# One first load for three x tiles, a cast moved to GpSimd, and the last stores cut in other places

## The chip, the cores and the metric

The kernel runs on one core of one Trainium2 chip. The metric is the device time of one execution in microseconds (us). The profile of an execution covers its span from the first to the last instruction, about 2 us less than the time. "Before" is the tuned kernel, "after" the same with the change. A DMA has "landed" when all the engines that move it have reported; each such report is a "landing mark".

## The reference

A batched matrix product with a bias and a residual. The batches fold into one matrix of 8192 x 1024.

```python
batch, m, k, n = 16, 512, 1024, 768
x: (batch, m, k)   weight: (k, n)   bias: (n)   residual: (batch, m, n)     # all float32
return (np.matmul(x, weight) + bias + residual).astype(np.float32)
```

## The kernel before

The 8192 rows are 64 tiles of 128 rows, and eight tiles make a "super tile" (S): partition p of super tile S holds eight neighbouring rows. For each tile, x is cast to bf16, transposed on TensorE in pairs (as fp32), copied back from PSUM (the memory that TensorE writes), multiplied in 16 matmuls, and finished by adds on VectorE and GpSimd. Almost every DMA is issued by SyncE on one queue, in the order of the program. The parts that the change and the argument touch:

```python
P, J, HEAD, X_BUFS, RO_BUFS, EARLY = 128, 8, 3, 2, 4, 24
...
    def store(S, j0=0, j1=J, n0=0, nl=N):
        K_(nc.sync.dma_start(
            out=out_d[S, :, j0:j1, n0:n0 + nl], in_=ro[S][:, j0:j1, n0:n0 + nl]
        ))
...
    load_x(0, 0, 2)          # tiles 0 and 1: 8 KB of each partition
    load_x(0, 2, 3)          # tile 2: 4 KB
    load_w(0)                # then four weight chunks, the rest of x, the residuals
...
    keep_warm(12)            # matmuls on zeros until x is there
    cast(0, "dve")
    cast(1)                  # ACT
    transp(0)
    transp(1)
    keep_warm(3)
    cast(2)                  # ACT
    transp(2)
    # then the bias is broadcast by four matmuls, then the first real matmuls
...
    for t in range(HEAD, n_t):
        ...
        if S == n_s - 1 and j == 0:
            store(S - 1)
        if S == n_s - 1 and j == J // 2:
            store(S, 0, J // 2)          # tiles 0-3 of the last super tile: 1536 KB
        if S == n_s - 1 and j == J - 1:
            store(S, J // 2, j)          # tiles 4-6: 1152 KB
    ...
        store(S, J - 1, J, n0, nl)       # tile 7: 256 KB and 128 KB
```

Of the kernel before, what the change touches and what calls it, by code (L numbers as in the profile page):

```python
# [11 lines left out]
J = 8  # L12
# [9 lines left out]
def kernel(  # L22
# [8 lines left out]
    nc = tc.nc  # L31
# [7 lines left out]
    n_s = n_t // J  # L39
# [12 lines left out]
    def ring(pool, name, i, n, shape, dt):  # L52
        return pool.tile(shape, dt, name=name, tag=f"{name}{i % n}", bufs=1)
# [8 lines left out]
    def load_x(S, j0=0, j1=J):  # L62
        if S < n_s:
            if j0 == 0:
                x_sb[S] = ring(sb, "x_tile", S, X_BUFS, [P, J, K], FP32)
            K_(nc.sync.dma_start(out=x_sb[S][:, j0:j1, :], in_=x_d[S, :, j0:j1, :]))

    def load_res(S, j0=0, j1=J):
        if S < n_s:
            if j0 == 0:  # L70
                ro[S] = ring(sb, "ro", S, RO_BUFS, [P, J, N], FP32)
            K_(nc.sync.dma_start(out=ro[S][:, j0:j1, :], in_=res_d[S, :, j0:j1, :]))

    def load_w(c):
        K_(nc.sync.dma_start(out=w_st[:, c, :, :], in_=w_d[:, c, :, :]))
# [7 lines that stand above are left out]
    def cast(t, engine="act"):  # L83
        if t < n_t:
            xb[t] = ring(sb, "xb", t, 4, [P, K], BF16)
            copy = nc.scalar.copy if engine == "act" else nc.vector.tensor_copy
            K_(copy(out=xb[t], in_=x_sb[t // J][:, t % J, :]))  # L87

    def transp(t):
        if t < n_t:  # L90

            pt = ring(ps, "pt", t, 2, [P, n_c, P], FP32)
            pairs = xb[t][:, :].bitcast(FP32)
            for c in range(n_c):
                K_(nc.tensor.transpose(  # L95
                    out=pt[:, c, :], in_=pairs[:, c * P:(c + 1) * P], identity=ident
                ))
            xt[t] = ring(sb, "xt", t, 4, [P, n_c, P], FP32)
            K_(nc.vector.tensor_copy(out=xt[t], in_=pt))  # L99
# [9 lines left out]
    def mms(t, i):  # L109
        if i == 0:  # L110
            po[t] = psum_o(t)
        for n0, nl in chunks:
            mm(t, i, n0, nl)
# [4 lines left out]
    def pool_add(t):  # L118
        if 0 <= t < n_t:
            r = row(t)  # L120
            K_(nc.gpsimd.tensor_add(out=r, in0=r, in1=tmp[t] if t < EARLY else bias_sb))  # L121

    def finish(t, n0=0, nl=N):
        if t < 0:
            return
        p = po[t][:, n0:n0 + nl]
        if t < EARLY:
            tmp[t] = ring(sb, "tmp", t, TMP_BUFS, [P, N], FP32)
            K_(nc.vector.tensor_add(out=tmp[t], in0=p, in1=bias_sb))  # L129
        else:  # L130
            K_(nc.vector.tensor_add(out=row(t, n0, nl), in0=p, in1=row(t, n0, nl)))  # L131
# [5 lines left out]
    w_st = ring(sb, "ro", RO_BUFS - 1, RO_BUFS, [P, n_c, 2, N], FP32)  # L137
    w_sb = const.tile([P, n_c, 2, N], BF16, name="w_sb")

    load_x(0, 0, 2)  # L140
    load_x(0, 2, 3)
    load_w(0)
    load_w(1)
    load_w(2)
# [23 lines left out]
    def keep_warm(n):  # L168
        for _ in range(n):
            K_(nc.tensor.matmul(  # L170
                warm_ps[:, 0:512], lhsT=warm[:, 0:P], rhs=warm, start=True, stop=True
            ))
# [5 lines left out]
            K_(nc.vector.tensor_copy(out=w_sb[:, c, e, :], in_=w_st[:, c, e, :]))  # L178


    keep_warm(12)
    cast(0, "dve")
    cast(1)
    transp(0)
    transp(1)
    keep_warm(3)
    cast(2)
    transp(2)
    for n0, nl in chunks:
        K_(nc.tensor.matmul(  # L190
# [23 lines left out]
    for t in range(HEAD, n_t):  # L214
        cast(t + 2)
        S, j = divmod(t, J)
        if (t + 2) % J == J - 1:
            load_x(S + X_BUFS)
            load_res(S + X_BUFS)
            if 1 <= S < n_s - 1:  # L220
                store(S - 1)
        if t < n_t - 1:
            for i in range(len(steps)):
                mms(t, i)
                if i == 0 and t >= n_t - J // 2:
                    finish(t - 1)
                if i == T_STEP:
                    transp(t + 1)
        if t < n_t - J // 2 or t == n_t - 1:
            finish(t - 1)  # L230
        if t - 1 < EARLY:
            pool_add(t - 1)
        if t + 1 >= EARLY:
            pool_add(t + 1)
        if S == n_s - 1 and j == 0:
            store(S - 1)
        if S == n_s - 1 and j == J // 2:
            store(S, 0, J // 2)
        if S == n_s - 1 and j == J - 1:
            store(S, J // 2, j)  # L240
    t, S = n_t - 1, n_s - 1
    for b, (n0, nl) in enumerate(chunks):
        po[t] = psum_o(t + b)
# [34 lines left out]
```

## Time and profile before

| | before |
|---|---|
| time, median of 3 runs | 211.06 us (210.88 to 211.19) |
| span of the profiled run | 209.1 us |
| first real matmul, last matmul's end | 10.04, 204.43 us |
| last store issued, last packet's end, last landing | 204.92, 207.78, 208.18 us |

First the page: busy time and share of the span of PE (TensorE's matmuls), and from the 40 equal slices the busy tenths of PE and of the 16 DMA engines.

```profile
PE 201.1 (96%) x1274; PEld 130.8 (63%) x1299; DVE 105.0 (50%) x139; ACT 68.0 (33%) x68; POOL 115.6 (55%) x71
...
PE   7999999999899999999999999999999999999991
...
DMA  6999999999999999999999999999999999999966
```

PE and DMA are both nearly full from beginning to end. Shares alone don't say which of the two decides. Next, groups of instructions: line, engine, operation, tiles and shapes, count, then busy us and mean ns of one, then the engine's idle time and what ended it.

```profile
L87 ACT CAST xb<-x_tile 128x1024 bf16<-128x1024 f32 x62 | 63.2, 1045 | 115.5 <-PE pt L95 63.2
L121 POOL TENSOR_TENSOR ro<-ro,bias_sb 128x768 f32<-128x768 f32 x40 | 71.2, 1816 | 34.6 <-DMA ro<-in_residual_dram 24.6
```

ACT casts a tile in 1.05 us, a GpSimd add takes 1.82 us, and both engines are idle for long.

The chain of waits, in order of time (start, us, what), around the only place where PE stands still for more than 0.14 us after its start:

```profile
22.74 33.22 DMA x_tile<-in_x_dram
...
56.05 1.05 ACT xb L87
...
57.15 0.66 PE pt L95 x4
```

The third x super tile is issued at 22.74 and lands only at 55.95 us, because the queue ahead of it is long. The cast follows, and then the transposition of tile 16. In the records of the transpositions each tile starts 3.037 us after the one before; tile 16 is 0.83 us late and tile 17 another 0.06. From there PE runs without a stall until 204.43.

The head, by the timeline (start, us, engine, line, operation, out<-in, count, idle before and what ended it):

```profile
5.62 1.04 ACT L87 CAST xb<-x_tile 128x1024 bf16<-128x1024 f32 x1 [2.11 <-DMA x_tile<-in_x_dram]
5.62 0.69 DVE L87 CAST xb<-x_tile 128x1024 bf16<-128x1024 f32 x1 [4.35 <-DMA x_tile<-in_x_dram]
...
6.87 1.05 ACT L87 CAST xb<-x_tile 128x1024 bf16<-128x1024 f32 x1 [0.20 <-DMA x_tile<-in_x_dram]
...
8.31 0.60 PE L95 MATMUL pt<-ident,xb 128*128 128x128 f32 x4
...
10.04 1.14 PE L104 MATMUL po<-w_sb,xt 128*128 128x512 bf16 x6
```

The two casts at 5.62 wait for the load of tiles 0 and 1, the cast at 6.87 for the load of tile 2. The first real matmul (line 104) starts at 10.04.

The tail, by DMA issue (KB, then us from issue to landing):

```profile
out_dram<-ro SPq DMA_DIRECT2D x1, 1536.0 KB, 10.4
out_dram<-ro SPq DMA_DIRECT2D x1, 1152.0 KB, 4.2
...
out_dram<-ro SPq DMA_DIRECT2D x1, 256.0 KB, 3.4
out_dram<-ro SPq DMA_DIRECT2D x1, 128.0 KB, 3.3
```

And by windows of half a microsecond; the last two columns are the mean busy share of the 16 DMA engines and what they moved:

```profile
202.50:203.00 0.50, 0.50 (x4) 0.23 (x3) 0.40 (x1) 0.00 (x0) 0.00 (x0) 1.00 0.12 49
203.00:203.50 0.50, 0.50 (x4) 0.26 (x3) 0.00 (x0) 0.00 (x0) 0.00 (x0) 1.00 0.12 49
...
206.50:207.00 0.50, 0.00 (x0) 0.00 (x0) 0.00 (x0) 0.00 (x0) 0.00 (x0) 1.00 0.82 311
207.00:207.50 0.50, 0.00 (x0) 0.00 (x0) 0.00 (x0) 0.00 (x0) 0.00 (x0) 1.00 1.03 369
207.50:208.00 0.50, 0.00 (x0) 0.00 (x0) 0.00 (x0) 0.00 (x0) 0.00 (x0) 1.00 0.33 107
```

A share of 0.12 is 2 of 16 engines. From 202.5 to 203.5 two engines still work while fourteen have nothing to do. The trace also has the 16 landing marks of each of these DMAs, one for each engine. They are the finest view that we have (us from the span's start, sorted):

```
before, store of tiles 0-3:      201.21 201.25 201.30 201.54 201.78 201.91 202.63 202.73 202.84 202.91 202.92 202.97 203.10 203.44 204.16 204.30
before, store of tiles 4-6:      206.92 ... 207.12
before, last store (128 KB):     207.95 ... 208.18
```

Six engines lead, eight are about 1.5 us behind them, two about 3 us. The two laggards never run dry: their last 12 KB packet of the first store ends at 203.83, and the 9 KB packets of the next follow until 206.75. The other fourteen begin the next store at 203.75, having waited for it. So here all engines happen to end together.

Among the packets are ten of 16,384 bytes that belong to no tensor but to the instruction stream, about one every 19 us, each of about 1.0 to 1.1 us on one engine. The Trainium skill ("Runtime: NRT & Kernel Launch", Instruction fetch mechanics) describes instruction refills in blocks of 16 KiB, 256 instructions; ten blocks agree with the 2,573 matmuls and weight loads of this trace. After the first such packet, at 21.98 us, one landing mark of the next DMA is 1.05 us behind the others; after the second there are two such marks, after the third three. But the fetches are not the whole lag. At the store of tiles 0 to 3 the lags behind the first engine add up to 21.6 us. At 20.6 us, before the first fetch, they were 3.7. The ten packets, with four more of 8 KB of the instruction stream, took 11.8 us, so at least about a third of the growth has another cause.

### The profile page before, as it was taken

The page shows a single profiled execution, that of the slowest core. Times are in us where ns is not written, and L with a number is a line of the kernel's source. Part 1 is how long each engine was busy: PE and PEld are TensorE (multiplying, and loading weights), DVE is VectorE, ACT ScalarE, POOL GpSimd, SP SyncE. Part 2 cuts the span into 40 slices and gives each one's busy share as a digit, 9 for nine tenths or more (in the row PEclk, how much of TensorE's full clock was granted, in tenths as well). Part 3 has the DMA queues.
Part 4 walks back from the last instruction along what each step waited for, and adds up shares of the span by engine and source line. Part 5 has one row for each costly group of instructions (what it writes and reads, how often), then busy time and mean ns, then how long its engine had stood idle before and what let it go on. Part 6 is the DMA issues. An engine that isn't in the chain of part 4 may idle for free.

```text
span 209.1 us, 3149 instructions
## 1 busy us (share of the span) xinstructions
PE 201.1 (96%) x1274; PEld 130.8 (63%) x1299; DVE 105.0 (50%) x139; ACT 68.0 (33%) x68; POOL 115.6 (55%) x71
## 2 busy tenths in 40 slices
PE   7999999999899999999999999999999999999991
PEld 2556666666566666666666666666666666666660
DVE  0646564455354455445545544554554455446551
ACT  2544315520283054323423252440543234322000
POOL 2000197819936655999499802994069900799000
PEclk9999999999999999999999999999999999999999
DMA  6999999999999999999999999999999999999966
GB/s 229 428 422 432 430 421 438 443 456 407 404 476 420 409 432 412 443 428 434 437 415 459 415 414 447 437 426 418 428 431 443 445 412 421 432 442 423 414 287 273
DMA packets 5344, 87.23 MB, mean 417 GB/s; under 512 B 593, under 2 KB 721, under 8 KB 1618
## 3 DMA queue, kind: packets, MB, share of 16 engines
q1 hardware_dynamic: 5328, 87.03, 97.8%
q8 instruction: 10, 0.16, 0.3%
q14 instruction: 4, 0.03, 0.0%
q10 hardware_dynamic: 2, 0.00, 0.0%
HBM read 61.87 MB, written 25.17 MB: 416 GB/s over the span
## 4 chain that ended last, share of the span: by engine, by line
PE 70%; DMA 25%; issue 1%; ACT 1%; DVE 0%; POOL 0%; ACTq 0%; POOLq 0%
PE po L104 60%; DMA x_tile<-in_x_dram 23%; PE pt L95 10%; DMA tmp<-in_bias_dram 2%; ACT xb L87 1%; DVE ro L131 0%; POOL ident masks.py:197 0%; ACTq L87 0%; POOL tmp L135 0%; POOLq L262 0%
## 5 line engine op out<-in xcount | busy, mean ns | idle before, releaser
L104 PE MATMUL po<-w_sb,xt 128*128 128x512 bf16 (+1 forms) x999 | 175.4, 324 | 1.4
L104 PEld LDWEIGHTS <-xt 128*128 128x128 bf16 x1024 | 100.1, 98 | 59.5 <-DVE xt L99 0.5
L87 ACT CAST xb<-x_tile 128x1024 bf16<-128x1024 f32 x62 | 63.2, 1045 | 115.5 <-PE pt L95 63.2
L121 POOL TENSOR_TENSOR ro<-ro,bias_sb 128x768 f32<-128x768 f32 x40 | 71.2, 1816 | 34.6 <-DMA ro<-in_residual_dram 24.6
L99 DVE COPY xt<-pt 128x512 f32<-128x512 f32 x64 | 44.2, 692 | 88.3 <-PE pt L95 88.2
L121 POOL TENSOR_TENSOR ro<-ro,tmp 128x768 f32<-128x768 f32 x24 | 43.1, 1816 | 42.3 <-DMA ro<-in_residual_dram 25.0
L131 DVE TENSOR_TENSOR ro<-po,ro 128x768 f32<-128x768 f32 (+2 forms) x41 | 38.0, 930 | 2.9 <-PE po L104 2.8
L95 PE MATMUL pt<-ident,xb 128*128 128x128 f32 x256 | 38.6, 274 | 0.7 <-ACT xb L87 0.7
L95 PEld LDWEIGHTS pt<-ident,xb 128*128 128x128 f32 x256 | 30.1, 142 | 9.2 <-ACT xb L87 1.3
L129 DVE TENSOR_TENSOR tmp<-po,bias_sb 128x768 f32<-128x768 f32 x24 | 22.8, 949 | 0.4 <-PE po L104 0.4
L170 PE MATMUL po<-warm 128*128 128x512 bf16 x15 | 6.1, 579 | 1.2 <-DVE warm L156 1.2
L176 ACT CAST w_sb<-ro 128x768 bf16<-128x768 f32 x4 | 3.3, 832 | 4.0 <-DMA ro<-in_weight_dram 4.0
L170 PEld LDWEIGHTS <-warm 128*128 128x128 bf16 x15 | 1.9, 132 | 4.1 <-issue 2.8
L87 DVE CAST xb<-x_tile 128x1024 bf16<-128x1024 f32 x2 | 1.4, 694 | 5.1 <-DMA x_tile<-in_x_dram 5.1
L178 DVE CAST w_sb<-ro 128x768 bf16<-128x768 f32 x4 | 2.2, 556 | 2.2 <-DMA ro<-in_weight_dram 2.2
L161 ACT ACT_TABLE_LOAD x1 | 1.3, 1283 | 2.0 <-POOL ident masks.py:199 2.0
L190 PE MATMUL po<-tmp 128*128 128x512 f32 (+1 forms) x4 | 1.5, 486 | 0.0
L198 DVE COPY bias_sb<-po 128x768 f32<-128x768 f32 x1 | 1.0, 958 | 0.1
L190 PEld LDWEIGHTS po<-tmp 128*128 128x128 f32 x4 | 0.7, 190 | 0.5 <-issue 0.5
L135 POOL MEMSET tmp<- 128x768 f32 x1 | 0.7, 737 | 0.3 <-POOLq L262 0.3
L156 DVE MEMSET warm<- 128x256 uint32 x1 | 0.3, 272 | 0.9 <-PEq L262 0.9
masks.py:199 POOL TENSOR_SCALAR_AFFINE_SELECT ident<-ident 128x128 f32<-128x128 f32 x1 | 0.3, 292 | 0.1
(8 smaller groups left out, 1.0 us busy)
## 6 DMA issues: line engine op xcount, KB each, us to landing
x_tile<-in_x_dram SPq DMA_DIRECT2D x6, 4096.0 KB, 29.4
ro<-in_residual_dram SPq DMA_DIRECT2D x7, 3072.0 KB, 18.0
out_dram<-ro SPq DMA_DIRECT2D x7, 3072.0 KB, 24.9
x_tile<-in_x_dram SPq DMA_DIRECT2D x2, 2048.0 KB, 23.9
x_tile<-in_x_dram SPq DMA_DIRECT2D x3, 1024.0 KB, 8.7
ro<-in_weight_dram SPq DMA_DIRECT2D x4, 768.0 KB, 9.1
ro<-in_residual_dram SPq DMA_DIRECT2D x2, 1536.0 KB, 20.9
out_dram<-ro SPq DMA_DIRECT2D x1, 1536.0 KB, 10.4
```

The costliest lines, as they stand in the source:

```text
L87: K_(copy(out=xb[t], in_=x_sb[t // J][:, t % J, :]))
L95: K_(nc.tensor.transpose(out=pt[:, c, :], in_=pairs[:, c * P:(c + 1) * P], identity=ident))
L99: K_(nc.vector.tensor_copy(out=xt[t], in_=pt))
L104: K_(nc.tensor.matmul(po[t][:, n0:n0 + nl], lhsT=both[:, e, :], rhs=w_sb[:, c, e, n0:n0 + nl], start=(i == 0), stop=(i == len(steps) - 1),))
L121: K_(nc.gpsimd.tensor_add(out=r, in0=r, in1=tmp[t] if t < EARLY else bias_sb))
L129: K_(nc.vector.tensor_add(out=tmp[t], in0=p, in1=bias_sb))
L131: K_(nc.vector.tensor_add(out=row(t, n0, nl), in0=p, in1=row(t, n0, nl)))
L161: K_(nc.scalar.copy(out=warm_a, in_=warm_a))
L170: K_(nc.tensor.matmul(warm_ps[:, 0:512], lhsT=warm[:, 0:P], rhs=warm, start=True, stop=True))
L176: K_(nc.scalar.copy(out=w_sb[:, c, e, :], in_=w_st[:, c, e, :]))
L178: K_(nc.vector.tensor_copy(out=w_sb[:, c, e, :], in_=w_st[:, c, e, :]))
L190: K_(nc.tensor.matmul(bias_ps[:, n0:n0 + nl], lhsT=ones, rhs=bias_row[:, n0:n0 + nl], start=True, stop=True,))
```

## The change

The intent: fewer and larger packets for the first tiles, with three engines casting at once; and at the end less left to store after the last matmul.

```diff
-    load_x(0, 0, 2)
-    load_x(0, 2, 3)
+    load_x(0, 0, 3)
...
-    keep_warm(12)
+    keep_warm(14)
     cast(0, "dve")
     cast(1)
     transp(0)
     transp(1)
-    keep_warm(3)
-    cast(2)
+    keep_warm(1)
+    cast(2, "pool")                      # nc.gpsimd.tensor_copy
     transp(2)
...
+        if S == n_s - 1 and j == J - 2:
+            store(S, J // 2, j)          # tiles 4 and 5: 768 KB
         if S == n_s - 1 and j == J - 1:
-            store(S, J // 2, j)
+            store(S, j - 1, j)           # tile 6: 384 KB
```

More of the change, by code (lines that the diff above doesn't have):

```diff
@@ L85, in cast @@
             xb[t] = ring(sb, "xb", t, 4, [P, K], BF16)
-            copy = nc.scalar.copy if engine == "act" else nc.vector.tensor_copy
+            copy = {
+                "act": nc.scalar.copy, "dve": nc.vector.tensor_copy,
+                "pool": nc.gpsimd.tensor_copy,
+            }[engine]
             K_(copy(out=xb[t], in_=x_sb[t // J][:, t % J, :]))
```

## The prediction

> **What bounds the kernel now.** Two resources are full at once. The page shows PE busy 96% and the DMA engines at 417 GB/s, slices at 9 almost throughout. The spacing of the transposes in the timeline is 3.04 us per tile with one exception: tile 16 starts 0.83 us late (plus 0.06 at the next). The chain of waits names the reason: the third x super tile lands at 55.95 us, although it was issued at 22.74 behind a full queue. After that PE never stalls and its last matmul ends at 204.4. The tail is DMA: the last store is issued at 204.92, its packets end at 207.8, it lands at 208.2.
>
> The finer reading is by DMA engine. In windows of half a microsecond the DMA share falls to 0.12 from 202.5 to 203.5: two of 16 engines still work off the 1.5 MB store of tiles 0 to 3 (12 KB packets of 0.461 us each), fourteen are idle. The landing marks of that store agree: 201.2 on the first engine, 204.2 and 204.3 on the last two. These two lag about 3 us; 16 KB instruction fetches of about 1.07 us each, found among the packets, explain at least part of it. From 203.9 they go straight on with the 1152 KB store until 206.8, then the two last pieces until 207.8. So the laggards have work without a break to the end. The Trainium skill ("DMA: Bandwidth & Descriptors", Queues, rings and completion order) says that each engine consumes its descriptors in ring order; the trace agrees.
>
> **Head of the change.** Three tiles in one load: an 8 KB and a 4 KB packet per row (0.309 + 0.161 us) become one of 12 KB (0.461), times 8 rows per engine: 0.07 us less. Tile 0 and 1 land at about 6.8 instead of 5.6. Casts: DVE 0.69 and ACT 1.05 us; the first two transpositions end at about 8.5 instead of 7.7, at the warm rate (0.44 us per tile). The GpSimd cast of 1024 elements: its 768-element memset takes 0.74 us and its two-input add 1.82; the skill ("GPSIMD Engine Reference", Engine selection) calls one-input work roughly line-rate. Estimate 1.0 to 1.7 us, perhaps more beside the DVE cast. So transposition of tile 2 starts at 8.7 to 9.1 instead of 8.3, bias matmuls (1.3 us) follow, and the first real matmul starts at about 10.5 (10.3 to 11.0) instead of 10.04. This loss of about 0.5 us is swallowed by the 0.89 us stall at tile 16, whose load is queue-bound and lands 0.07 us earlier. PE ends at 204.4 as before.
>
> **Tail of the change.** Tiles 4 and 5 (768 KB) are issued at about 199.9 instead of 202.9 and fill the fourteen idle engines. The two laggards only get the same bytes in other pieces: 8 x (0.235 + 0.121) instead of 8 x 0.356 us. They end at 207.7 to 207.8 as before. Gain about zero; the last store's issue has 1.6 us of slack on them.
>
> **Predicted time:** 211.0 us, 80% range 210.5 to 211.5. Faster by over 2%: 0.01; within 2%: 0.98; slower: 0.01.
>
> **What would show it.** Right: first matmul near 10.5, the stall at tile 16 shrunk to about 0.4 us, PE ending near 204.4, DMA share near 0.12 to 0.2 in the last half microsecond of packets (before: 14 to 16 engines together), landing marks of the last stores spread by over 1 us (before: 0.2), last landing still near 208.1. Wrong on the tail: last landing near 207 with all engines done together.
>
> **What would make it wrong.** The fetches falling on other engines, so that the laggards lag less (up to 1 us faster); a GpSimd cast of over 2.5 us (slower); the idle engines' absence speeding up the laggards' packets.

## The result, and the profile after

After takes 210.98 us (median of 6 runs, 210.89 to 211.20), before in the same rounds 211.01 us. The ratio is 1.000, with a 95% interval of 0.9987 to 1.0013. The span is 209.2 us.

The head, by the timeline:

```profile
6.74 0.69 DVE L90 CAST xb<-x_tile 128x1024 bf16<-128x1024 f32 x1 [5.47 <-DMA x_tile<-in_x_dram]
6.74 1.05 ACT L90 CAST xb<-x_tile 128x1024 bf16<-128x1024 f32 x1 [3.23 <-DMA x_tile<-in_x_dram]
6.77 1.56 POOL L90 CAST xb<-x_tile 128x1024 bf16<-128x1024 f32 x1 [4.79 <-DMA x_tile<-in_x_dram]
...
9.09 0.63 PE L98 MATMUL pt<-ident,xb 128*128 128x128 f32 x4 [0.22 <-DVE xt L102]
...
10.85 0.70 PE L107 MATMUL po<-w_sb,xt 128*128 128x512 bf16 x3
```

All three casts start together, 1.1 us later than the first two did. The GpSimd cast takes 1.56 us. The transposition of tile 2 starts at 9.09 instead of 8.31, and the first real matmul at 10.85 instead of 10.04. Between these two traces the head has lost 0.81 us. Other traces put the loss higher: e2 and h2 below have the head of before and start at 9.74 and 9.56, and the seven other traces with the unaltered new head start at 10.94 to 11.10. In the trace of before the transpositions of tiles 0 and 1 started 0.76 us apart, in e2 0.47.

The GpSimd cast was not what tile 2 waited for. It ended at 8.33. The transposition came at 9.09, after VectorE had copied tile 0 out of the PSUM buffer that tile 2 uses next (8.25 to 8.94).

Around tile 16, by the timeline:

```profile
54.10 0.60 PE L98 MATMUL pt<-ident,xb 128*128 128x128 f32 x4
...
56.25 1.99 ACT L90 CAST xb<-x_tile 128x1024 bf16<-128x1024 f32 x2 [12.56 <-DMA x_tile<-in_x_dram]
...
57.35 0.42 PEld L98 LDWEIGHTS pt<-ident,xb 128*128 128x128 f32 x4 [0.44 <-ACT xb L90]
```

Tile 16 starts 3.25 us after tile 15, so the stall is 0.22 us where it was 0.83. The x super tile lands at 56.15 us, 0.20 later than before. The two differences add up to the 0.81 us that the head lost: PE ends at 204.63, later by no more than the landing.

The tail, by DMA issue and by windows:

```profile
out_dram<-ro SPq DMA_DIRECT2D x1, 768.0 KB, 6.3
...
out_dram<-ro SPq DMA_DIRECT2D x1, 384.0 KB, 4.2
out_dram<-ro SPq DMA_DIRECT2D x1, 256.0 KB, 3.4
out_dram<-ro SPq DMA_DIRECT2D x1, 128.0 KB, 3.1
```

```profile
202.50:203.00 0.50, 0.50 (x4) 0.25 (x3) 0.50 (x1) 0.00 (x0) 0.00 (x0) 1.00 0.89 369
203.00:203.50 0.50, 0.50 (x4) 0.24 (x3) 0.10 (x1) 0.00 (x0) 0.00 (x0) 1.00 0.68 283
...
206.50:207.00 0.50, 0.00 (x0) 0.00 (x0) 0.00 (x0) 0.00 (x0) 0.00 (x0) 1.00 0.22 80
207.00:207.50 0.50, 0.00 (x0) 0.00 (x0) 0.00 (x0) 0.00 (x0) 0.00 (x0) 1.00 0.12 47
207.50:208.00 0.50, 0.00 (x0) 0.00 (x0) 0.00 (x0) 0.00 (x0) 0.00 (x0) 0.84 0.07 23
```

The idle hole between 202.5 and 203.5 is mostly filled. Now the hole is at the end: from 207.0 two engines work, then one. The landing marks:

```
after, store of tiles 4-5:       203.17 203.19 203.22 203.34 203.60 203.64 204.23 204.51 204.54 204.56 204.69 204.77 204.87 205.45 206.10 206.42
after, last store (128 KB):      206.78 206.78 206.79 206.81 206.82 206.82 206.83 206.85 206.87 206.92 206.94 206.96 206.98 207.38 207.99 208.25
```

Thirteen engines are done with the last store by 206.98, a microsecond earlier than before. The last mark is at 208.25, where it was 208.18. The stores of the change are early for most engines and worth nothing to the two that end last.

### The profile page after: what moved, and what is told of

It is laid out like the page before. It is cut to its first block, busy times and chain, and to the rows that moved or that the text cites. A ratio compares the mean times of both kernels' runs of the same rounds, so it can differ in the third digit from the quotient of the medians.

```text
span 209.2 us, 3149 instructions
## 1 busy us (share of the span) xinstructions
PE 201.1 (96%) x1274; PEld 130.6 (62%) x1299; DVE 104.8 (50%) x139; ACT 67.0 (32%) x67; POOL 117.2 (56%) x72
## 4 chain that ended last, share of the span: by engine, by line
PE 70%; DMA 25%; issue 1%; ACT 1%; DVE 0%; ACTq 0%; SPq 0%
PE po L107 60%; DMA x_tile<-in_x_dram 25%; PE pt L98 10%; ACT xb L90 1%; DVE ro L134 0%; ACTq L90 0%; SPq L66 0%
## 5 line engine op out<-in xcount | busy, mean ns | idle before, releaser
L90 ACT CAST xb<-x_tile 128x1024 bf16<-128x1024 f32 x61 | 62.2, 1045 | 116.7 <-PE pt L98 84.9
L90 POOL CAST xb<-x_tile 128x1024 bf16<-128x1024 f32 x1 | 1.6, 1557 | 4.8 <-DMA x_tile<-in_x_dram 4.8
```

Of the source, the lines that this page charges most:

```text
L90: K_(copy(out=xb[t], in_=x_sb[t // J][:, t % J, :]))
```

## The experiments

The theory: the end is the time at which the slowest DMA engine has worked off its own queue. The change gives that engine the same bytes. The late start of PE is absorbed by the stall at tile 16, and the rest of any delay by the laggards' backlog. Rival 1: two real effects cancel, a loss of 0.8 us at the head and an equal win at the tail. Rival 2: the end of PE plus a fixed latency of the last store decides. Runs of different submissions went to different chips, so each is compared with its own runs of before (medians 211.34, 211.27 and 211.37 us).

### Each half alone

e1 is after with the tail of before, e2 is before with the tail of after.

```diff
 e1 (from after)                              e2 (from before)
-        if ... j == J - 2:                  +        if ... j == J - 2:
-            store(S, J // 2, j)             +            store(S, J // 2, j)
         if ... j == J - 1:                           if ... j == J - 1:
-            store(S, j - 1, j)              -            store(S, J // 2, j)
+            store(S, J // 2, j)             +            store(S, j - 1, j)
```

> The one load of three tiles with the GpSimd cast, and the store pieces of the kernel before. Theory (two lagging DMA engines end last and the late start of PE is swallowed by the stall at tile 16): within 0.2 us of the kernel before, first real matmul at 10.8 to 10.9, PE ending at 204.4 to 204.7, last landing 208.1 to 208.4. Rival (two real effects that cancel: a head that loses 0.8 us and a tail that wins 0.8 us): 0.4 to 0.9 us slower than before.

> The head of the kernel before, and the new store pieces. Theory of the lagging engines: within 0.15 us of the kernel before; in the trace fourteen engines are done with the last store by about 207 and two at about 208.1 to 208.3. Rival (effects that cancel): 0.4 to 0.9 us faster than before.

e1: 211.41 us, ratio 0.9999 (0.9986 to 1.0012); first real matmul at 10.94, PE ending at 204.52, last landing 208.62. e2: 211.39 us, ratio 1.0007 (0.9988 to 1.0027); thirteen engines done with the last store by 207.16, the fourteenth at 207.58, the last two at 208.41 and 208.48. Each half alone is worth nothing: rival 1 falls. The last landings were 0.2 us later than the expected ranges in both, so a few tenths of a microsecond between two traces mean little.

e2 also shows the stall at work unasked. In that run the same head as in before started its first matmul at 9.74, 0.3 us earlier, and the stall at tile 16 grew to 1.31 us: PE only waited longer for a load that landed at 56.25.

### A later PE, in both kernels

Warming matmuls ahead of the first real one delay PE and change nothing else.

```diff
 e3 (from after):   -    keep_warm(1)    +    keep_warm(8)
 e4 (from before):  -    keep_warm(3)    +    keep_warm(10)
 f4 (from before):  -    keep_warm(3)    +    keep_warm(14)
```

> The kernel after with seven more warming matmuls (7 x 0.216 = 1.5 us of PE) ahead of the first real one. Theory of the lagging engines: the stall at tile 16 gives back its last 0.22 us, PE ends about 1.3 us later (about 205.9), the last store is issued about 1.3 us later, but the two engines have work queued until then: last landing at most 0.2 us later and the time within 0.25 us of the kernel before. Rival (the end of PE plus a fixed latency of the last store decides): 1.2 to 1.4 us slower.

> The kernel before with the same seven warming matmuls. Theory of the lagging engines: the stall at tile 16 swallows 0.83 of 1.5 us, PE ends about 0.65 us later, and here the store of tiles 4 to 6 is one piece issued only after that: the laggards run dry at 203.9 and wait about 0.5 us for it. So 0.4 to 0.7 us slower than before, more than the kernel after loses by the same delay. Rival (the end of PE plus a fixed latency): 0.65 us slower here and 1.3 us in the kernel after, the other way round.

> The kernel before with eleven more warming matmuls, so that PE ends where it ended in the late kernel after, at about 205.5. Theory: the one-piece store of tiles 4 to 6 is then issued at about 204.0, all engines are idle until then, and the last landing moves from 208.2 to about 209.2: 0.8 to 1.2 us slower than before, where the kernel after with the same end of PE lost nothing. Rival (the end of PE plus a fixed latency): the same for both, which the late kernel after already contradicts; within 0.3 us would mean that the split of the store bought no slack.

| | first matmul | PE ends | last store issued | last landing | ratio to before |
|---|---|---|---|---|---|
| before | 10.04 | 204.43 | 204.92 | 208.18 | 1 |
| after | 10.85 | 204.63 | 205.12 | 208.25 | 1.0000 (0.9987 to 1.0013) |
| e3, after, late | 12.08 | 205.59 | 206.08 | 208.34 | 0.9989 (0.9973 to 1.0004) |
| e4, before, late | 11.18 | 204.69 | 205.18 | 208.45 | 1.0006 (0.9988 to 1.0025) |
| f4, before, later | 12.01 | 205.52 | 206.01 | 209.27 | 1.0035 (1.0022 to 1.0047) |

e3 and f4 are the pair to look at: PE ends within 0.07 us of the same time. In the kernel after the last store is issued 0.96 us later than without the delay and lands 0.09 us later. (1.3 us were expected; the first 0.4 us of warming filled a wait for the copy of tile 0 that was there already.) In the kernel before the last landing moves by 1.09 us, in the timed runs by 0.74 us (212.01 against 211.27). Rival 2 falls: with the same end of PE the two end 0.9 us apart. The expectation for e4 was too large, because the first matmul moved by 1.14 us and not by 1.5: the first two tiles' transpositions ended 0.37 us earlier than in the profiled run of before, at 0.11 us each from the start. Of 1.14 us the stall swallowed 0.89, PE ended 0.26 us later, and the landing moved by 0.27. f4 came out just below its range in time, inside it in the trace.

The windows of f4 show where the microsecond goes:

```profile
203.50:204.00 0.50, 0.50 (x4) 0.20 (x3) 0.48 (x1) 0.00 (x0) 0.00 (x0) 1.00 0.06 25
204.00:204.50 0.50, 0.50 (x4) 0.21 (x3) 0.00 (x0) 0.00 (x0) 0.00 (x0) 1.00 0.00 0
...
208.50:209.00 0.50, 0.00 (x0) 0.00 (x0) 0.00 (x0) 0.00 (x0) 0.00 (x0) 1.00 0.51 170
```

From 204.0 to 204.5 no DMA engine moves anything: the store of tiles 4 to 6, in one piece, is not issued before 204.01. The same for e3:

```profile
203.00:203.50 0.50, 0.50 (x4) 0.22 (x3) 0.40 (x1) 0.00 (x0) 0.00 (x0) 1.00 1.01 418
203.50:204.00 0.50, 0.50 (x4) 0.26 (x3) 0.50 (x1) 0.00 (x0) 0.00 (x0) 1.00 0.78 320
...
207.50:208.00 0.50, 0.00 (x0) 0.00 (x0) 0.00 (x0) 0.00 (x0) 0.00 (x0) 1.00 0.13 45
```

No hole there before the end: tiles 4 and 5 were in the queue. So the split does what it was meant for. It buys about a microsecond of slack for PE that this kernel has no use for.

### Which engines are late

Small loads into a dead buffer, behind the store of tiles 0 to 3, serve as a roll call. The Trainium skill ("DMA: Bandwidth & Descriptors", Why a DMA increments its semaphore by 16 and not by 1) says that a DMA from SyncE uses the largest number of engines, up to 16, that divides its row count, the lowest-numbered ones. The counts agree: loads of 1, 2, 4 and 8 rows had 1, 2, 4 and 8 late landing marks, and the rows of the later calls did as well. That these are the lowest-numbered engines is the page's word; the marks show only how many there are, and fit sets that are nested.

```diff
 (from after)
         if S == n_s - 1 and j == J // 2:
             store(S, 0, J // 2)
+            for m, p in enumerate((1, 2, 4, 8)):        # f1; g1: 10, 12, 14, 15; g2: 5, 6, 7, 13
+                # p rows of 4 KB into the x buffer of super tile 6, which nothing reads any more
+                K_(nc.sync.dma_start(out=x_flat[0:p, m * K:m * K + K], in_=...))
```

> A look, not a comparison: behind the store of tiles 0 to 3 of the last super tile four small loads into a dead buffer, of 1, 2, 4 and 8 rows of 4 KB, which the Trainium skill says run on that many lowest-numbered engines. Their landing marks tell how late the engines 0, 1, 2-3, 4-7 are at about 202 to 205 us. Theory of the lagging engines: the marks of the 16 engines form the three groups seen before (leaders, about 1.5 us behind, about 3 us behind), and each small load lands at its engines' times, not all at once. Rival (the queue as a whole is late, no engine of its own): all four land within 0.3 us of one another on all their engines.

> A look: the first roll call found the two laggards in none of the engines 0 to 7. Four small loads of 10, 12, 14 and 15 rows at the same place. The load of 14 rows has no mark near 204.5 if the laggards are engines 14 and 15; it has one if one of them is 8 to 13; the load of 15 rows has one mark near 204.6 if 15 is one of two. The end of the kernel stays within 0.2 us of the kernel after.

> A look for the last two names: small loads of 5, 6, 7 and 13 rows. The second roll call put one laggard at engine 14 and the other at 12 or 13; the first put the third-slowest engine (0.7 us ahead of the laggards) among 4 to 7. If the load of 13 rows has a mark near 204.5, the other laggard is engine 12, if none, engine 13. If the loads of 5, 6 and 7 rows have no mark near 203.9 to 204.2, the third-slowest is engine 7. The end of the kernel stays within 0.2 us of the kernel after.

```
f1, store of tiles 0-3:  201.16 201.31 201.63 201.68 201.74 201.75 202.48 202.78 202.85 202.94 202.94 202.99 203.01 203.74 204.44 204.47
f1,  1 row:   201.34
f1,  2 rows:  201.54 202.17
f1,  4 rows:  201.73 202.03 202.37 203.12
f1,  8 rows:  201.52 201.91 202.34 202.55 202.69 203.14 203.31 203.94
g1, 12 rows:  201.53 201.76 201.84 202.60 202.81 202.97 203.10 203.42 203.57 203.63 203.80 204.02
g1, 14 rows:  201.75 201.94 202.09 202.82 202.86 203.04 203.18 203.41 203.64 203.82 203.83 204.05 204.23 204.54
g2,  5 rows:  201.67 202.29 202.40 203.44 203.89
g2, 13 rows:  201.44 201.62 202.73 202.79 203.04 203.11 203.16 203.21 203.28 203.36 203.47 204.01 204.50
```

A small load on an engine lands when that engine gets to it: 201.34 on the first, 203.94 on the slowest of the first eight. The queue as a whole is not late, single engines are, and the rival of f1 falls. Each load adds 0.16 to 0.21 us to the engines that it uses, so marks within one kernel shift from load to load. The load of 12 rows has no mark at the laggards' time; that of 14 has one, 204.54, whose engine is not among the first 12. In g2 the slowest mark of 5 rows, 203.89, moves to 204.50 with its fourth load, and no other of the first 13 is near it. (By the rule written down before g2, a mark near 204.5 would have named engine 12. The rule forgot that four loads move the third-slowest engine there.) So one laggard is engine 13. The other is 14 or 15; the marks of 15 rows in g1, which end with 204.43, 204.44 and 204.71, fit 14. The third-slowest is engine 4. All three looks took 210.97 to 211.20 us, single runs that count for nothing more.

### Work for one engine, and the same work for all

f2 adds 96 KB behind the store of tiles 0 to 3 as three rows of 32 KB, each moved by one engine, the first; f3 adds 96 KB at the same place as 16 rows of 6 KB, one for each engine. Both are 0.11% of the kernel's bytes.

```diff
 (from after, behind store(S, 0, J // 2))
+            for p in range(3):                           # f2
+                K_(nc.sync.dma_start(out=x_flat[p:p + 1, 0:8192], in_=...))
+            K_(nc.sync.dma_start(out=x_flat[0:16, 0:1536], in_=...))     # f3
```

> The kernel after with three loads of one 32 KB row each at the same place, 96 KB that one engine has to move (about 3 x 1.2 us = 3.7 us of its time, estimated from 0.92 us for 24 KB packets). Theory of the lagging engines: that engine ends last, and the time grows by 3.7 us less its lead over the two laggards: +3.7 if it is one of them, about +2.3 if of the middle group, about +0.7 if a leader; PE ends as before. Rival (the end of PE plus a fixed latency, or the bandwidth of all engines together): at most +0.25 us.

> The same 96 KB at the same place as 16 rows of 6 KB, one for each engine (0.235 us a packet). Theory of the lagging engines: the two laggards carry one packet more and the time grows by 0.2 to 0.3 us. Rival (fixed latency after PE): 0.

```
f2, the three loads:   202.67   203.89   205.10
f2, last store:        207.37 207.39 207.41 207.41 207.43 207.44 207.44 207.45 207.46 207.49 207.53 207.57 207.57 208.01 208.21 208.87
f3, last store:        206.84 206.85 206.87 206.89 206.90 206.91 206.91 206.92 206.92 206.93 206.95 206.97 207.00 207.67 208.12 208.51
```

In f2 each row takes its engine 1.22 us. The first engine, a leader in the roll call, becomes the last one: its marks go on at 206.96, 207.89, 208.54 and 208.87, each a store's own packets further. That is 0.62 us beyond the last landing of after and 0.66 beyond the laggard that was last before it, as the theory said for a leader (0.7). PE ended at 204.66, as in after. In f3 the last mark is 208.51, 0.26 later than in after. The times do not confirm the sizes: f2 211.52 us, ratio 1.0010 (0.9996 to 1.0024), so 0.2 us more than before and at most 0.5, where 0.7 was expected; f3 211.18 us, ratio 0.9999 (0.9986 to 1.0011), where 0.2 to 0.3 more was expected. After itself was not timed on that chip. For f2 the marks settle which engine ends last: one engine, the one that got the work, 0.66 us behind all others. f3 stays undecided, since its 0.26 us is no more than the differences between traces above.

### An attempt to win the time that the laggards cost

If engines 13 and 14 end last, they should get less. The 3 MB store of super tile 6 goes out in three pieces of 112, 13 and 3 rows, so that engines 13 to 15 move 7 rows instead of 8 and engines 0 to 2 move 9.

```diff
 h1 (from after), h2 (from before)
         if S == n_s - 1 and j == 0:
-            store(S - 1)
+            for p0, p1 in ((0, 112), (112, 125), (125, 128)):
+                K_(nc.sync.dma_start(out=out_d[S - 1, p0:p1], in_=ro[S - 1][p0:p1]))
```

> The roll calls name the late engines: 13 and 14 (about 3 us behind the leaders), then 4 (0.7 us ahead of those two), the others at least 1.4 us ahead. Here the 3 MB store of super tile 6 goes out as 112, 13 and 3 rows instead of 128: engines 13 to 15 carry 7 rows of 24 KB instead of 8 (0.92 us less), engines 0 to 2 carry 9, the others 8. Theory of the lagging engines: engine 4 ends last, about 0.65 us earlier than the laggards did; last landing at about 207.5 to 207.7, time 0.4 to 0.8 us below the kernel before, PE ending as in the kernel after. Rivals (fixed latency after PE, total bandwidth): no change.

> The same three pieces in the kernel before. Theory: there all engines wait until 203.8 for the one-piece store of tiles 4 to 6 and end together at 207.8 to 207.9, so taking work off the late engines gains nearly nothing: within 0.2 us of the kernel before. If instead the pieces themselves help, it gains as much as in the kernel after.

Both expectations failed, and badly. h1: 215.72 us, ratio 1.0208 (1.0194 to 1.0222). h2: 215.27 us, ratio 1.0179 (1.0165 to 1.0192). PE ended at 204.89 and 204.54, so the 4 us are DMA's. Windows of four microseconds, h1 first and then after:

```profile
194.00:198.00 4.00, 4.00 (x29) 2.73 (x27) 2.00 (x4) 0.00 (x0) 0.00 (x0) 1.00 1.24 369
198.00:202.00 4.00, 4.00 (x27) 2.59 (x26) 2.34 (x3) 0.00 (x0) 0.00 (x0) 1.00 0.88 206
```

```profile
194.00:198.00 4.00, 3.95 (x28) 2.77 (x28) 2.00 (x4) 0.00 (x0) 0.00 (x0) 1.00 1.01 433
198.00:202.00 4.00, 4.00 (x28) 2.59 (x26) 2.07 (x3) 0.00 (x0) 0.00 (x0) 1.00 0.93 396
```

From 198 to 202 the engines of h1 are busy 0.88 of the time and move 206 GB/s; those of after, busy 0.93, move 396. Some packets got very slow: those of 24 KB took 1.32 us on average from 194 to 198 and 2.18 from 198 to 202, the longest 5.7; in after 0.92. From 194 to 198, 46 of the 59 still took less than 1.4 us. On 16 engines 112 rows come to seven each, so other engines than usual should move these rows. The skill ("DMA: Bandwidth & Descriptors", The descriptor swizzle) says that in a transfer to 128 partitions each engine writes one port of the on-chip memory. A store reads that memory, so it is only a guess that here two engines met at one port. No run shows that; it stays open. What is shown is that this way of taking work off the laggards costs more than their lag, so the theory's share in it (what would be won if the packets kept their speed) was not tested.

No run changed the number of fetches. So that the fetches cause much of the lag is supported by sizes and times only: ten packets of about 1.0 to 1.1 us, and marks that fall behind by 1.05 us, one more after each of the first three.

No version beat either kernel.

## Why the prediction was right

- **The time.** Predicted 211.0 us, range 210.5 to 211.5; measured 210.98.
- **The bound.** Right: two engines with a backlog end last. e1, e2, e3, f2 and the landing marks show it. The identity (13, and probably 14) was not predicted.
- **The head.** First matmul predicted near 10.5 (10.3 to 11.0), measured 10.85. The loss was put at 0.5 us and came to 0.81, or more by the other traces; that cost nothing because of the stall and the slack below. The GpSimd cast was estimated at 1.0 to 1.7 us and took 1.56, 1.5 ns an element. The skill's "roughly line-rate" for one-input work ("GPSIMD Engine Reference", Engine selection) would be nearer the low end; the memsets of this trace, 0.205 us for 128 and 0.737 for 768 elements, come to 0.83 ns an element. A VectorE cast ran beside it for 0.69 us, so the cast alone was not measured.
- **The stall at tile 16.** Right in kind: it shrank from 0.83 to 0.22 us (predicted about 0.4) and PE ended 0.20 us later (predicted: no later). The term that was off is the x landing, predicted 0.07 us earlier and measured 0.20 later. With the head of before it was at 55.95, 56.02, 56.06, 56.25 and 56.26 in five profiled runs, with the head of after at 56.04 to 56.41 in nine, so 0.07 us is below what one trace can show.
- **The tail.** Right: DMA share 0.12 and 0.07 in the last two half microseconds with packets, marks of the last store spread over 1.47 us where it was 0.23, last landing 208.25 (predicted near 208.1).
- **The slack.** The 1.6 us that the prediction gave the last store were confirmed as far as they were tried: 0.96 us of delay cost 0.09 us of landing in e3, less than the differences between traces.
- **What would have made it wrong** did not happen. Two engines were 2.9 to 3.6 us behind the first at the store of tiles 0 to 3 in all traces whose stores had 128 rows, the GpSimd cast stayed under 2.5 us, and the last 12 KB packet of before took 0.46 us, like the others, though fourteen engines were idle.

## What to carry to other kernels

When all 16 DMA engines are busy to the end, look at the landing marks of one DMA: here the time ended with the slowest engines' own queues, and issuing the last pieces earlier only made the others finish earlier. An even share of bytes was not an even finish, but pieces with another row count than 128 made the packets more than twice as slow on average for a while, so a correction has to be measured. A stall that waits for a queue-bound load swallowed what was lost ahead of it, and in e2 what was won too, so read the head's worth at that stall and not at its first matmul.

## What the Trainium skill lacked or had wrong

- "Runtime: NRT & Kernel Launch" (Instruction fetch mechanics) calls the cost of crossing a 16 KiB boundary mostly hidden. For PE it was: no stall of its own goes with a fetch. But each of the ten packets held a DMA engine for about 1.0 to 1.1 us, a landing mark fell behind by 1.05 us after the first, and by the end two engines were 3 us late, in part through fetches. That fetches and tensor data share the 16 engines follows from the queue model of another page ("DMA: Bandwidth & Descriptors", Queues, rings and completion order), which gives the refills a queue row of their own; what that costs the data stands on neither.
- "DMA: Bandwidth & Descriptors" (Latency and other measured facts) has engines 7 and 15 as the usual slow ones, with a guess at the cause that concerns DMAs issued by GpSimd. Here SyncE issues them, and by that page's own numbering the slow ones were 13, probably 14, and then 4.
- The same page has a rule for the engine count of 112 or 13 rows, but not what such pieces cost: 24 KB packets of 1.32 and 2.18 us on average instead of 0.92, and 4 us on the kernel.
- "GPSIMD Engine Reference" (Engine selection) has one-input work at roughly line-rate. A cast of 1024 fp32 elements to bf16 took 1.56 us, 1.5 ns an element, next to a VectorE cast. Whether the page is wrong is not shown: its own account of cycles an element has slower cases too.
- No page gives the spread of issue times seen here: the twelve small loads of the three roll calls took SyncE 0.55 to 1.18 us each, the stores of 128 rows in the same stretch 0.33 to 0.37. Few engines are not the whole reason: f3's load on all 16 took 1.10, and the last store of before 1.02. The reason stays open.
